# Hybrid decoder block with 32 experts: eight weight buffers over the merged activations, expert outputs as 128 rows of 1024

## The chip, the cores and the metric
The kernel runs on one core of a Trainium2 chip. Its time is the device time of one execution in microseconds, median of several runs. The core has five engines with queues of their own: TensorE (PE, with its weight loads as PEld), VectorE (DVE), ScalarE (ACT), GpSimd (POOL) and SyncE (SP), which here only issues DMA transfers. Sixteen DMA engines move data between HBM and SBUF.

## The reference
Input x has 512 tokens of width 2048, in float32. The block computes, in this order:

```
xn = rmsnorm(x);  proj = xn @ w_in
fox = forgetting attention (8 heads of 128);  ret = retention (8 heads of 128), group norm, gated
merged = sum over the two branches of sigmoid(gates) * (branch @ w_branch)
h = x + merged @ w_out
hn = rmsnorm(h)
group = argmax of 4 group logits; in it, the top 2 of 8 experts; weights = p_group * normalised top 2
moe[token] = sum over its 2 experts of weight * ((silu(hn @ w1[e]) * (hn @ w3[e])) @ w2[e])
out = rmsnorm(h + moe)
```

There are 32 experts. w1[e] and w3[e] are 2048 x 512, w2[e] is 512 x 2048, all float32: 12.58 MB for one expert, 402.7 MB for all.

## The kernel before, in words
The first part works through 60 pieces of 2 MB of dense weights, two "units" of 128 x 2048 at a time: a load of 2 MB into one of two `raw` buffers, a split of each unit by ACT and DVE into a rounded high part and the rest (`split`, two buffers named `whl`), three matmuls for each pair of tiles. The last dense product is `merged @ w_out` (L594 to L596). It goes over four column groups c of 512; in each over four quarters g of the inner dimension, then over the four token tiles. Its other operand are the merged activations `mh[k]` and `ml[k]`, k = 0 to 15, 32 tiles of 2 KB per partition at the right end of SBUF. Quarter g uses k = 4g to 4g + 3; the last column group is c = 3. Beside it and behind it run the residual, the transposes and the router's logits (tiles `hc`, `hh`, `hl`, `wrs`, `lg`), and then a chain of small DVE operations that gives each token its experts and its place (`rank1`).

The experts follow (loop from L882), each with 64 slots for tokens. `prep(e)` gathers an expert's tokens with matmuls by a 0/1 matrix S (L714 `ax`, L724 `gp`) and writes `xs`. `gemm1(e)` multiplies them by w1 (rows 0 to 63 of `ab`) and w3 (rows 64 to 127) in two halves g; each half needs two pieces of 2 MB. It then scales, transposes (`tr`) and gates to `gs`. `gemm2(e)` takes two pieces of w2: for each it runs 32 / 2 = 16 recorded matmuls into a PSUM tile `y`, and copies its two halves of 64 rows by ACT (L800) and DVE (L798) into `ysb`, 64 rows of 2048, of which there is one. GpSimd then scatters the rows by an indirect DMA to `ybuf` in DRAM (L803). The program's order is gemm1(0), prep(1), gemm1(1), prep(2), gemm2(0), gemm1(2), and so on; the last expert's gemm2 is not scattered but weighted and kept as `ys`, rounded part and rest.

A planner orders the instructions of PE, DVE, ACT and POOL by modelled times, so that work whose operands it expects early is drawn ahead; SP alone keeps the order of the program. All expert pieces are loaded from SP at L811, each into the next of seven buffers in a fixed cycle: two `raw`, three `r0` to `r2` (pool `raw2`), two `whl`. A load waits until the last reader of what its buffer overlays is done, and all that is behind it on SP waits too. `raw2` lies in space that the router's tiles used before.

At the end `combine` loads `ybuf` in four pieces of 2 MB (L918), for which the last scatter must have landed, adds the residual, the weighted rows and the last expert by matmuls (L930 to L933) and DVE (L934, L937), normalises and stores (L954). `fw` is the final norm's weight, spread over the partitions; `dgs` (L904) holds diagonal matrices of weights and shares a tile with `ab`. A loop for experts with more than 64 tokens stands behind it.

Of the kernel before, what the change touches and what calls it, by code (L numbers as in the profile page):

```python
# [30 lines left out]
DE = 512  # L31
SLOTS = 64
MAXBLK = 15
NR2 = 3
EPS = 1e-6
NEG = -1e30
ROPE_BASE = 10000.0
# [90 lines left out]
def hybrid_block(ctx, tc, a, out):  # L128
# [330 lines left out]
    scA.close()  # L459
    scM = ExitStack()  # L460
    mp = scM.enter_context(pool("mT", 1, side="right", reuse_waits="tile"))
    mh = [mp.tile([P, T], F32R, name=f"mh{j}") for j in range(KT)]
    ml = [mp.tile([P, T], F32R, name=f"ml{j}") for j in range(KT)]
    with pool("mtmp", 2, reuse_waits="tile") as mt:
        for j in range(KT):
            hi, lo = unit("br", j, after=done[3] if j == 1 else None)
            gs, bs = [], []
            for n in range(2):
# [4 lines left out]
                for k in range(H):  # L473
# [28 lines left out]
    br = rp[0].tile([P, NR], F32, name="br")  # L502
    nc.gpsimd.dma_start(br, bcast_rows(a["b_router"], 0, NR))
    tok2 = rp[0].tile([P, NT], F32, name="tok2")
    nc.gpsimd.iota(tok2, pattern=[[2 * P, NT]], base=0, channel_multiplier=0,
                   allow_small_or_imprecise_dtypes=True)
    par2 = rp[0].tile([P, NT], F32, name="par2")
    nc.gpsimd.iota(par2, pattern=[[0, NT]], base=0, channel_multiplier=2,
                   allow_small_or_imprecise_dtypes=True)
    aux = rp[0].tile([P, NT, 40], BF, name="aux")  # L510
    nc.gpsimd.memset(aux[:, :, 5:8], -4096.0)
    nc.gpsimd.tensor_copy(aux[:, :, 3], tok2)
    nc.gpsimd.tensor_copy(aux[:, :, 4], par2)

# [176 lines left out]


    cp = scC.enter_context(pool("cx", 2, reuse_waits="tile"))
    raw2 = scC.enter_context(pool("raw2", 1, reuse_waits="tile"))
    slots = [(raw, "wraw")] * 2 + [(raw2, f"r{i}") for i in range(NR2)] + [(split, "whl")] * 2
    loads = itertools.cycle(slots)

    def buffer(shape=(P, 4096)):

        pl, tag = next(loads)  # L700
        return pl.tile(list(shape), F32, name="wraw", tag=tag)

    gathering = []

    def prep(rsel, is2, eng, late=False):

        S = cp.tile([P, NT, P], BF, name="S")
        for t in range(NT):
            i = eng.tensor_scalar(S[:, t], slot1.rearrange("p a b -> p (a b)"), rsel[:, t:t + 1], None,  # L709
                                  op0=OP.is_equal)  # L710
        gathering.append(i.ins)
        ax = psY.tile([P, 40], F32, name="ax", tag="y")
        for t in range(NT):
            nc.tensor.matmul(ax, S[:, t], aux[:, t], start=(t == 0), stop=(t == NT - 1))  # L714
        rs = cp.tile([P, 1], F32, name="rs", bufs=3)
        nc.vector.reduce_sum(rs, ax[:, 0:3], axis=AX.X)
        xs = cp.tile([P, KT, SLOTS], F32, name="xs")
        for g in range(2):
            ks = slice(8 * g, 8 * g + 8)
            gp = psG.tile([P, 8, SLOTS], F32, name="gp")  # L720
            for d in range(8):
                for t in range(NT):
                    for i in range(3):
                        nc.tensor.matmul(gp[:, d], h3[i][:, t, (8 * g + d) * P:(8 * g + d + 1) * P],  # L724
                                         S[:, t, :SLOTS], start=(t == 0 and i == 0),
                                         stop=(t == NT - 1 and i == 2))
            nc.vector.tensor_mul(xs[:, ks], gp, b3(nfw[:, ks, None], 8, SLOTS))  # L727
        if late:
            ws = psY.tile([P, 3], F32, name="ws", tag="y")
# [12 lines left out]
        nc.vector.reduce_sum(ix, ax[:, 3:6], axis=AX.X)  # L742
        nc.vector.scalar_tensor_tensor(idx, ix, 4096.0, is2(ax[:, 8:40]), op0=OP.add, op1=OP.add)
        return xs, rs, idx

    def halves_mm(acc, st, w, first, last):
# [25 lines left out]
    last_ins = []  # L772
    yp = []

    def gemm2(blk, pieces, late=False, ysb=None):

        gs, idx = blk
        if late:
            wsl, sT = idx
            ys = yp[0].tile([P, D], F32R, name="ys", tag="ysb")  # L780
        elif ysb is None:
            ysb = yp[0].tile([SLOTS, D], F32, name="ysb")
        for q in range(2):
            w = next(pieces)
            y = psY.tile([P, DE], F32, name="y")
            for k in range(4):
                halves_mm(y, gs[:, k], [w[:, (4 * m + k) * DE:(4 * m + k + 1) * DE] for m in range(2)],
                          k == 0, k == 3)
            for m in range(2):
                ym = y[m * SLOTS:(m + 1) * SLOTS]  # L790
                cs = slice((2 * q + m) * DE, (2 * q + m + 1) * DE)
                if late:
                    yt = cp.tile([SLOTS, DE], F32, name="yt", tag="xs")
                    nc.scalar.activation(yt, ym, AF.Copy, scale=wsl[m * SLOTS:(m + 1) * SLOTS])
                    nc.scalar.copy(ys[:SLOTS, cs], yt)
                    nc.vector.tensor_sub(ys[SLOTS:, cs], yt, ys[:SLOTS, cs].bitcast(F32))
                elif m:
                    nc.vector.tensor_copy(ysb[:, cs], ym)  # L798
                else:
                    nc.scalar.copy(ysb[:, cs], ym)  # L800
        if late:
            return sT, ys
        nc.gpsimd.indirect_dma_start(  # L803
            out=ybuf, out_offset=IndirectOffsetOnAxis(ap=idx[:SLOTS, :1], axis=0),
            in_=ysb, in_offset=None, bounds_check=2 * T - 1, oob_is_err=False)

    def pieces_of(we, part):

# [72 lines left out]
    prev = None  # L881
    for e in range(NE):  # L882
        if e == NE - 1:
            fw = yp[0].tile([P, D], F32, name="fw")
            gemm2(prev, pieces_of(a["wM"][e - 1], 1))
            spread_fw(fw)
        cur = gemm1(x0, pieces_of(a["wM"][e], 0))
        if e == 8:
            with tc.issue_after(last_ins[-1].ins):
                nblk, eid, sta, en, it = extra_blocks()  # L890
        if e == 12:
            with tc.issue_after(last_ins[-1].ins):
# [12 lines left out]
        return dgs  # L905

    dgs = diagonals()
    sT, ys = gemm2(prev, pieces_of(a["wM"][NE - 1], 1), True)


    yv = ybuf.rearrange("(t p k) d -> t p k d", p=P, k=2)
# [48 lines left out]
    with tc.If(n_extra > 0):  # L960
        with tc.For_i(0, n_extra, 1):
            ind, tmp, e1, base = f("ind", NE), f("tmp", NE), f("e1", 1), f("base", 1)
            nc.vector.tensor_scalar(ind, sta, it, None, op0=OP.is_le)
            nc.vector.tensor_scalar(tmp, en, it, None, op0=OP.is_gt)
            nc.vector.tensor_mul(ind, ind, tmp)
            nc.vector.tensor_mul(tmp, ind, iota32)
            nc.vector.reduce_sum(e1, tmp, axis=AX.X)
            nc.vector.tensor_copy(eid, e1)
            nc.vector.tensor_mul(tmp, ind, sta)
            nc.vector.reduce_sum(base, tmp, axis=AX.X)  # L970
            nc.vector.tensor_sub(base, it, base)
            nc.vector.tensor_scalar(base, base, 1.0, float(SLOTS), op0=OP.add, op1=OP.mult)
            rsel, tmp4 = f("rsel", NT), f("tmp4", NT, NE)
            nc.vector.tensor_mul(tmp4, rank1, b3(ind[:, None, :], NT, NE))
            nc.vector.reduce_sum(rsel, tmp4, axis=AX.X)
            nc.vector.tensor_scalar(rsel, rsel, base, None, op0=OP.subtract)
            nc.vector.tensor_scalar_add(it, it, 1.0)

            def is2(c):
                nc.vector.tensor_mul(tmp, c, ind)  # L980
                r = cp.tile([P, 1], F32, name="is2")
                nc.vector.reduce_sum(r, tmp, axis=AX.X)
                return r

            ev = nc.values_load(eid[0:1, 0:1], engines=[mybir.EngineType.SP], min_val=0, max_val=NE - 1)

            we = a["wM"][ds(ev, 1)].rearrange("e q p n -> (e q) p n")
            gemm2(gemm1(prep(rsel, is2, nc.vector), pieces_of(we, 0)), pieces_of(we, 1), False, buffer((SLOTS, D)))
        combine(diagonals())
    scC.close()  # L990

# [69 lines left out]
```

## Time and profile before
| what | value |
|---|---|
| median of 3 runs | 2466.49 us (2464.05 to 2470.78) |
| profiled execution | 2463.99 us, its span 2462.3 us |
| mean granted TensorE clock | 0.989 |
| PE busy | 2374.6 us (96%) |
| DVE, ACT, POOL busy | 735.9, 484.8, 232.9 us |
| HBM read, written | 562.72 MB, 37.24 MB |
| expert loads | 192 of 2048 KB, median 22.4 us from issue to landing |

The span begins with the first instruction of the profiled execution; all times below count from there. Rows of the profile name a line (L749), an engine, an operation and `output<-input` by the program's tile names. An engine's idle time is put down to what ended it, after `<-`. In the strips of 40 slices each digit is a share in tenths; a slice is 61.6 us.

### The profile page before, as it was taken

The numbers are of one execution on the slowest core, as the hardware profiler recorded it, in microseconds if no ns is written. First come the engines' busy times: TensorE is split into PE (matmuls) and PEld (weight loads), VectorE is DVE, ScalarE is ACT, GpSimd is POOL, SyncE is SP. The second block draws the span as 40 slices with busy tenths as digits, with TensorE's granted clock in tenths as the row PEclk, the third lists the DMA queues.
The fourth block names the chain that finished last, engine by engine and source line by source line (L and its number), as shares of the span: only waits on it lengthen the run. The fifth ranks groups of instructions, "written<-read, shape, count | busy, mean of one in ns | idle before, by whom it ended". The sixth has DMA issues, their size and how long they took to land. (4 is left out here: it accounts for less than half of the span.)

```text
span 2462.3 us, 36017 instructions
## 1 busy us (share of the span) xinstructions
PE 2374.6 (96%) x16110; PEld 1618.9 (66%) x16114; DVE 735.9 (30%) x1269; ACT 484.8 (20%) x617; POOL 232.9 (9%) x328
## 2 busy tenths in 40 slices
PE   8999999999999999999999979999999999999896
PEld 6888888888888888888888855544444444444332
DVE  4444445544452222244433231111111111111105
ACT  5222222222222222232223210000001000000003
POOL 0000000100000000000003121111111111111002
PEclk9999999999999999999999989999999999999998
DMA  7233333222223333244432369999999999999995
GB/s 291 96 107 129 107 104 136 82 107 73 107 80 126 128 124 127 102 147 154 146 125 94 128 286 425 382 424 426 427 425 426 426 427 426 426 425 426 426 410 219
DMA packets 69455, 594.22 MB, mean 241 GB/s; under 512 B 7800, under 2 KB 24248, under 8 KB 34640
## 3 DMA queue, kind: packets, MB, share of 16 engines
q1 hardware_dynamic: 40320, 549.48, 54.6%
q0 software_dynamic: 7856, 25.61, 3.1%
q10 hardware_dynamic: 21120, 16.78, 2.1%
q8 instruction: 128, 2.10, 0.3%
q14 instruction: 31, 0.25, 0.0%
HBM read 562.72 MB, written 37.24 MB: 244 GB/s over the span
## 5 line engine op out<-in xcount | busy, mean ns | idle before, releaser
L749 PE MATMUL ab<-wraw,xs 128*64 128x512 f32 x2048 | 490.7, 602 | 26.8 <-DMA wraw<-in_wM_dram 26.8
L226 PE MATMUL acc<-xh,whl 128*128 128x512 f32 x1152 | 453.8, 394 | 0.0
L228 PE MATMUL acc<-xh,whl 128*128 128x512 f32 x1152 | 453.7, 394 | 0.0
L227 PE MATMUL acc<-xl,whl 128*128 128x512 f32 x1152 | 453.3, 393 | 0.0
L97 ACT CAST whl<-wraw 128x2048 fp32r<-128x2048 f32 (+1 forms) x122 | 228.1, 1869 | 780.4 <-PE acc L228 412.4
L749 PEld LDWEIGHTS ab<-wraw,xs 128*64 128x64 f32 x2048 | 150.3, 138 | 312.6 <-issue 272.9
L98 DVE TENSOR_TENSOR whl<-wraw,whl 128x2048 fp32r<-128x2048 f32 (+1 forms) x122 | 275.3, 2257 | 202.0 <-ACT whl L97 201.7
L749 PE MATMUL y<-wraw,gs 128*64 128x512 f32 x1024 | 270.1, 599 | 1.7 <-DVE gs L769 0.9
L227 PEld LDWEIGHTS acc<-xl,whl 128*128 128x128 f32 x1152 | 216.5, 188 | 46.4 <-issue 1.4
L228 PEld LDWEIGHTS acc<-xh,whl 128*128 128x128 f32 x1152 | 216.5, 188 | 46.0 <-issue 1.4
L226 PEld LDWEIGHTS acc<-xh,whl 128*128 128x128 f32 x1152 | 216.6, 188 | 45.3 <-issue 0.5
L724 PEld LDWEIGHTS <-h 128*128 128x128 bf16 x6144 | 186.7, 98 | 31.3 <-issue 30.2
L724 PE MATMUL gp<-S,h 128*128 128x64 bf16 x6144 | 191.4, 194 | 12.9 <-issue 12.9
L749 PEld LDWEIGHTS y<-wraw,gs 128*64 128x64 f32 x1024 | 85.6, 137 | 137.5 <-issue 134.3
L727 DVE TENSOR_TENSOR xs<-gp,nfw 128x512 f32<-128x512 f32 x64 | 41.8, 687 | 406.5 <-PE ab L749 368.2
L709 POOL TENSOR_SCALAR S<-slot,rank 128x128 bf16<-128x128 f32 x124 | 73.1, 600 | 707.0 <-PE ax L714 632.0
L762 ACT ACTIVATE ab<-ab,rs 128x512 f32<-128x512 f32 x32 | 22.0, 687 | 503.9 <-PE ab L749 486.1
L243 PE MATMUL acc<-whl,xh 128*128 128x512 f32 x256 | 101.6, 401 | 6.1 <-ACT xh L202 6.1
L244 PE MATMUL acc<-whl,xh 128*128 128x512 f32 x256 | 102.4, 400 | 1.0 <-DVE whl L98 1.0
L594 PE MATMUL acc<-whl,mh 128*128 128x512 f32 x256 | 100.6, 393 | 0.0
L595 PE MATMUL acc<-whl,mh 128*128 128x512 f32 x256 | 100.3, 392 | 0.0
L478 PE MATMUL acc<-oh,whl 128*128 128x512 f32 x256 | 99.5, 390 | 0.6 <-DVE whl L86 0.6
(300 smaller groups left out, 2057.3 us busy)
## 6 DMA issues: line engine op xcount, KB each, us to landing
wraw<-in_wM_dram SPq DMA_DIRECT2D x192, 2048.0 KB, 22.4
wraw<-in_wA_dram SPq DMA_DIRECT2D x59, 2048.0 KB, 7.9
ybuf<-zero ACTq DMA_DIRECT2D x8, 1024.0 KB, 5.9
gate<-gs ACTq DMA_DIRECT2D x32, 256.0 KB, 2.0
g<-gate POOLq DMA_DIRECT2D x32, 256.0 KB, 3.0
wraw<-ybuf SPq DMA_DIRECT2D x4, 2048.0 KB, 14.4
xt<-in_x_dram SPq DMA_DIRECT2D x4, 1024.0 KB, 6.7
hc<-in_x_dram POOLq DMA_DIRECT2D x4, 1024.0 KB, 5.5
```

Of the source, the lines that this page charges most:

```text
L97: nc.scalar.copy(hi[:, c], w[:, c])
L98: nc.vector.tensor_sub(lo[:, c], w[:, c], hi[:, c].bitcast(F32))
L226: nc.tensor.matmul(acc, wh, xh[:, k], start=(k == 0), stop=False)
L227: nc.tensor.matmul(acc, wh, xl[:, k], start=False, stop=False)
L228: nc.tensor.matmul(acc, wl, xh[:, k], start=False, stop=(k == KT - 1))
L243: nc.tensor.matmul(accs[t], xh[:, k, s], wh, start=(k == 0), stop=False)
L244: nc.tensor.matmul(accs[t], xh[:, k, s], wl, start=False, stop=False)
L478: nc.tensor.matmul(b, wl, oh[i], start=False, stop=(k == H - 1))
L594: nc.tensor.matmul(accs[t], mh[k][:, s], wh, start=(k == 0), stop=False)
L595: nc.tensor.matmul(accs[t], mh[k][:, s], wl, start=False, stop=False)
L724: nc.tensor.matmul(gp[:, d], h3[i][:, t, (8 * g + d) * P:(8 * g + d + 1) * P], S[:, t, :SLOTS], start=(t == 0 and i == 0), stop=(t == NT - ...
L749: nc.tensor.matmul(acc[m * SLOTS:(m + 1) * SLOTS], st, w[m], start=first, stop=last)
```

## The change
The seven buffers become eight: `raw2` gets four buffers, placed at the right end over `mh` and `ml`, and the cycle is r3, r2, r1, raw, raw, r0, whl, whl. The merged activations are allocated from the last to the first, so that r3 lies over k = 0 to 3, r2 over 4 to 7, r1 over 8 to 11 and r0 over 12 to 15. `fw` and `ys` are each taken from this cycle for good before the last two experts, and six buffers are left for the loads behind.

`gemm2` takes both of its pieces first. Piece m holds the columns from 1024 m on, and `y` number q now has in its rows 0 to 63 columns of piece 0 and in rows 64 to 127 columns of piece 1. One copy of 128 x 512 each (ACT for q = 0, DVE for q = 1) fills `ysb`, 128 rows of 1024, and the scatter writes 128 rows of 4 KB where it wrote 64 of 8 KB; its row numbers are made for both halves. `is2`, `tok2` and `par2` are scaled for that, and `rowbase` adds the half's number.

```diff
-    mh = [mp.tile([P, T], F32R, name=f"mh{j}") for j in range(KT)]
-    ml = [mp.tile([P, T], F32R, name=f"ml{j}") for j in range(KT)]
+    mh, ml = ([None] * KT for _ in range(2))
+    for j in reversed(range(KT)):
+        mh[j] = mp.tile([P, T], F32R, name=f"mh{j}")
+        ml[j] = mp.tile([P, T], F32R, name=f"ml{j}")
...
-    raw2 = scC.enter_context(pool("raw2", 1, reuse_waits="tile"))
-    slots = [(raw, "wraw")] * 2 + [(raw2, f"r{i}") for i in range(NR2)] + [(split, "whl")] * 2
-    loads = itertools.cycle(slots)
-
-    def buffer(shape=(P, 4096)):
-
-        pl, tag = next(loads)
-        return pl.tile(list(shape), F32, name="wraw", tag=tag)
+    raw2 = scC.enter_context(pool("raw2", 1, side="right", reuse_waits="tile"))
+    loads = itertools.cycle([(raw2, "r3"), (raw2, "r2"), (raw2, "r1"), (raw, "wraw"), (raw, "wraw"), (raw2, "r0"),
+                             (split, "whl"), (split, "whl")])
+    kept = set()
+    for i in range(4):
+        raw2.tile([P, 4096], F32, name="wraw", tag=f"r{i}")
+
+    def buffer(shape=(P, 4096), dtype=F32, keep=False):
+
+        pl, tag = next(x for x in loads if x[1] not in kept)
+        if keep:
+            kept.add(tag)
+        return pl.tile(list(shape), dtype, name="wraw", tag=tag)
...
-        nc.vector.scalar_tensor_tensor(idx, ix, 4096.0, is2(ax[:, 8:40]), op0=OP.add, op1=OP.add)
+        nc.vector.tensor_add(ix, ix, rowbase)
+        nc.vector.scalar_tensor_tensor(idx, is2(ax[:, 8:40]), 2.0, ix, op0=OP.mult, op1=OP.add)
...
-    def gemm2(blk, pieces, late=False, ysb=None):
+    def gemm2(blk, pieces, ys=None):
...
-            ys = yp[0].tile([P, D], F32R, name="ys", tag="ysb")
-        elif ysb is None:
-            ysb = yp[0].tile([SLOTS, D], F32, name="ysb")
+        else:
+            ysb = yp[0].tile([P, 2, DE], F32, name="ysb")
+        w = [next(pieces), next(pieces)]
         for q in range(2):
-            w = next(pieces)
             y = psY.tile([P, DE], F32, name="y")
             for k in range(4):
-                halves_mm(y, gs[:, k], [w[:, (4 * m + k) * DE:(4 * m + k + 1) * DE] for m in range(2)],
-                          k == 0, k == 3)
+                ws = slice((4 * q + k) * DE, (4 * q + k + 1) * DE)
+                halves_mm(y, gs[:, k], [w[m][:, ws] for m in range(2)], k == 0, k == 3)
+            if ys is None:
+                if q:
+                    nc.vector.tensor_copy(ysb[:, q], y)
+                else:
+                    nc.scalar.copy(ysb[:, q], y)
+                continue
...
         nc.gpsimd.indirect_dma_start(
-            out=ybuf, out_offset=IndirectOffsetOnAxis(ap=idx[:SLOTS, :1], axis=0),
-            in_=ysb, in_offset=None, bounds_check=2 * T - 1, oob_is_err=False)
+            out=ybuf.rearrange("r (m n) -> (r m) n", m=2),
+            out_offset=IndirectOffsetOnAxis(ap=idx[:, :1], axis=0),
+            in_=ysb.rearrange("p q n -> p (q n)"), in_offset=None, bounds_check=4 * T - 1, oob_is_err=False)
...
         if e == NE - 1:
-            fw = yp[0].tile([P, D], F32, name="fw")
+            fw = buffer((P, D), F32, True)
+            ys = buffer((P, D), F32R, True)
             gemm2(prev, pieces_of(a["wM"][e - 1], 1))
```

## Rows read from the trace of the kernel before
**Rows 1.** The page: TensorE's busy time; DMA engines' share and rate in 40 slices

```profile
PE 2374.6 (96%) x16110; PEld 1618.9 (66%) x16114; DVE 735.9 (30%) x1269; ACT 484.8 (20%) x617; POOL 232.9 (9%) x328
...
DMA  7233333222223333244432369999999999999995
GB/s 291 96 107 129 107 104 136 82 107 73 107 80 126 128 124 127 102 147 154 146 125 94 128 286 425 382 424 426 427 425 426 426 427 426 426 425 426 426 410 219
```

**Rows 2.** Stretches: each engine's busy us, then granted clock, DMA share, GB/s

```profile
1437.00:1457.00 20.00, 14.79 (x241) 10.10 (x243) 6.78 (x28) 0.00 (x0) 4.87 (x8) 0.77 1.00 425
1540.00:1580.00 40.00, 40.00 (x522) 20.66 (x520) 4.18 (x9) 2.11 (x4) 5.63 (x9) 1.00 0.90 358
1700.00:2000.00 300.00, 288.90 (x2979) 135.00 (x2977) 42.58 (x126) 24.94 (x45) 32.93 (x50) 1.00 1.01 426
...
2390.00:2405.00 15.00, 13.95 (x61) 4.53 (x58) 0.23 (x1) 1.41 (x3) 0.00 (x0) 0.94 0.63 267
```

**Rows 3.** Waits of SP's queue, 1370 to 1500: total us, times, longest

```profile
SPq L811 <- DVE hl L554: 27.6, 1, 27.6
```

**Rows 4.** Expert loads (L811) in 1378:1434, 1434:1450, 1450:1470; landing in 1370:1500

```profile
L811 SPq DMA_DIRECT2D wraw<-in_wM_dram x2: 327/328/328, 1378.8 to 1404.3; - x2
...
L811 SPq DMA_DIRECT2D wraw<-in_wM_dram x5: 327/383/644, 1434.5 to 1436.6; - x5
...
L811 SPq DMA_DIRECT2D wraw<-in_wM_dram x4: 328/353/384, 1457.1 to 1464.4; - x4
...
DMA to landing us min/median/max: 7.6/13.6/26.3
```

**Rows 5.** L596, last column group, quarters 1, 2 and 4: first and last start

```profile
L596 PE MATMUL acc<-whl,ml x16: 388/390/396, 1387.8 to 1398.9; 128*128 128x512 f32 x16
L596 PE MATMUL acc<-whl,ml x16: 388/390/390, 1399.6 to 1409.8; 128*128 128x512 f32 x16
L596 PE MATMUL acc<-whl,ml x17: 388/390/401, 1410.5 to 1422.3; 128*128 128x512 f32 x17
```

**Rows 6.** Timeline of PE, first experts: start us, us, what, count

```profile
1450.03 13.95 PE L749 MATMUL ab<-wraw,xs 128*64 128x512 f32 x64
...
1470.17 13.96 PE L749 MATMUL ab<-wraw,xs 128*64 128x512 f32 x64
...
1491.71 6.23 PE L749 MATMUL y<-wraw,gs 128*64 128x512 f32 x28 [0.30 <-issue]
```

**Rows 7.** The gather's matmuls (L724) alone in two stretches of 30 us

```profile
1540.00:1570.00 30.00, 12.58 (x396) 11.96 (x396) 1.00 0.90 366
1600.00:1630.00 30.00, 5.76 (x192) 5.74 (x192) 1.00 1.00 422
```

**Rows 8.** PE's groups, 1600 to 2300: busy, mean ns, idle before

```profile
L749 PE MATMUL y<-wraw,gs 128*64 128x512 f32 x736 | 197.3, 596 | 0.4 <-issue 0.4
```

**Rows 9.** DMA queues in 1600:2300, 2437:2462, 1000:1300: packets, MB, share

```profile
q0 software_dynamic: 1920, 6.05, 2.1%
...
q1 hardware_dynamic: 1152, 4.19, 42.4%
...
q0 software_dynamic: 2944, 9.75, 10.5%
```

**Rows 10.** Timelines of POOL, ACT, DVE and PE near the end

```profile
2405.16 2.35 POOL L904 TENSOR_SCALAR dgs<-ident,wt 128x128 f32<-128x128 f32 x4 [30.53 <-PE tr L765]
2407.68 0.93 POOL L803 DMA_INDIRECT ybuf<-ysb,idx  x1 [0.17 <-issue]
...
2404.18 1.04 ACT L800 COPY ysb<-y 64x512 f32<-64x512 f32 x2
...
2404.77 1.30 DVE L798 COPY ysb<-y 64x512 f32<-64x512 f32 x2 [31.32 <-ACT ysb L800]
...
2420.77 0.75 DVE L934 SCALAR_TENSOR_TENSOR wraw<-wraw,wt,ab 128x512 f32<-128x512 f32 x1 [3.34 <-DMA wraw<-ybuf]
...
2406.58 7.09 PE L749 MATMUL y<-wraw,gs 128*64 128x512 f32 x32 [0.95 <-DVE gs L769]
```

More of the change, by code (lines that the diff above doesn't have):

```diff
@@ L33 @@
 MAXBLK = 15
-NR2 = 3
 EPS = 1e-6
@@ L504, in hybrid_block @@
     tok2 = rp[0].tile([P, NT], F32, name="tok2")
-    nc.gpsimd.iota(tok2, pattern=[[2 * P, NT]], base=0, channel_multiplier=0,
+    nc.gpsimd.iota(tok2, pattern=[[4 * P, NT]], base=0, channel_multiplier=0,
                    allow_small_or_imprecise_dtypes=True)
     par2 = rp[0].tile([P, NT], F32, name="par2")
-    nc.gpsimd.iota(par2, pattern=[[0, NT]], base=0, channel_multiplier=2,
+    nc.gpsimd.iota(par2, pattern=[[0, NT]], base=0, channel_multiplier=4,
                    allow_small_or_imprecise_dtypes=True)
     aux = rp[0].tile([P, NT, 40], BF, name="aux")
-    nc.gpsimd.memset(aux[:, :, 5:8], -4096.0)
+    nc.gpsimd.memset(aux[:, :, 5:8], -8192.0)
     nc.gpsimd.tensor_copy(aux[:, :, 3], tok2)
@@ L693, in hybrid_block @@
     cp = scC.enter_context(pool("cx", 2, reuse_waits="tile"))
-    raw2 = scC.enter_context(pool("raw2", 1, reuse_waits="tile"))
-    slots = [(raw, "wraw")] * 2 + [(raw2, f"r{i}") for i in range(NR2)] + [(split, "whl")] * 2
-    loads = itertools.cycle(slots)
-    def buffer(shape=(P, 4096)):
-        pl, tag = next(loads)
-        return pl.tile(list(shape), F32, name="wraw", tag=tag)
+    raw2 = scC.enter_context(pool("raw2", 1, side="right", reuse_waits="tile"))
[9 more added lines that the diff above has]
+        return pl.tile(list(shape), dtype, name="wraw", tag=tag)
     gathering = []
+    rowbase = rp[0].tile([P, 1], F32, name="rowbase")
+    nc.gpsimd.memset(rowbase[:SLOTS], 8192.0)
+    nc.gpsimd.memset(rowbase[SLOTS:], 8193.0)
     def prep(rsel, is2, eng, late=False):
@@ L773, in hybrid_block @@
     yp = []
-    def gemm2(blk, pieces, late=False, ysb=None):
+    def gemm2(blk, pieces, ys=None):
         gs, idx = blk
-        if late:
+        if ys is not None:
             wsl, sT = idx
-            ys = yp[0].tile([P, D], F32R, name="ys", tag="ysb")
-        elif ysb is None:
-            ysb = yp[0].tile([SLOTS, D], F32, name="ysb")
+        else:
+            ysb = yp[0].tile([P, 2, DE], F32, name="ysb")
+        w = [next(pieces), next(pieces)]
         for q in range(2):
-            w = next(pieces)
@@ L789, in gemm2 @@
             for m in range(2):
                 ym = y[m * SLOTS:(m + 1) * SLOTS]
[L791 to L800, printed above, removed]
@@ L801, in gemm2 @@
-        if late:
-            return sT, ys
+                cs = slice((2 * m + q) * DE, (2 * m + q + 1) * DE)
+                yt = cp.tile([SLOTS, DE], F32, name="yt", tag="xs")
+                nc.scalar.activation(yt, ym, AF.Copy, scale=wsl[m * SLOTS:(m + 1) * SLOTS])
+                nc.scalar.copy(ys[:SLOTS, cs], yt)
+                nc.vector.tensor_sub(ys[SLOTS:, cs], yt, ys[:SLOTS, cs].bitcast(F32))
+        if ys is not None:
+            return sT
         nc.gpsimd.indirect_dma_start(
-            out=ybuf, out_offset=IndirectOffsetOnAxis(ap=idx[:SLOTS, :1], axis=0),
-            in_=ysb, in_offset=None, bounds_check=2 * T - 1, oob_is_err=False)
+            out=ybuf.rearrange("r (m n) -> (r m) n", m=2),
+            out_offset=IndirectOffsetOnAxis(ap=idx[:, :1], axis=0),
+            in_=ysb.rearrange("p q n -> p (q n)"), in_offset=None, bounds_check=4 * T - 1, oob_is_err=False)
@@ L907, in hybrid_block @@
     dgs = diagonals()
-    sT, ys = gemm2(prev, pieces_of(a["wM"][NE - 1], 1), True)
+    sT = gemm2(prev, pieces_of(a["wM"][NE - 1], 1), ys)
     yv = ybuf.rearrange("(t p k) d -> t p k d", p=P, k=2)
@@ L972, in hybrid_block @@
             nc.vector.tensor_scalar(base, base, 1.0, float(SLOTS), op0=OP.add, op1=OP.mult)
-            rsel, tmp4 = f("rsel", NT), f("tmp4", NT, NE)
+            rsel, tmp4 = f("rsel", NT), oh1.rearrange("p t g j -> p t (g j)")
             nc.vector.tensor_mul(tmp4, rank1, b3(ind[:, None, :], NT, NE))
@@ L987, in hybrid_block @@
             we = a["wM"][ds(ev, 1)].rearrange("e q p n -> (e q) p n")
-            gemm2(gemm1(prep(rsel, is2, nc.vector), pieces_of(we, 0)), pieces_of(we, 1), False, buffer((SLOTS, D)))
+            gemm2(gemm1(prep(rsel, is2, nc.vector), pieces_of(we, 0)), pieces_of(we, 1))
         combine(diagonals())
```

## The prediction
> **What bounds the kernel now.** I read the page's first two parts first. TensorE is busy for 96% of the span, but the DMA strip says more: about 1420 of the 2462 us have the DMA engines at two to four tenths, and from slice 24 on (each is 61.6 us) they stand at 9 and move 425 GB/s [rows 1]. So there are two kernels in one: dense projections bound by TensorE, then the experts, bound by the load of their weights. An expert's six loads are 12.58 MB and its rows written to ybuf about 0.26 MB (1024 rows of 8 KB over 32 experts); at 426 GB/s that is 30.2 us, of which TensorE is idle for 1.1 us (288.9 of 300 us busy, over 300 / 30.2 = 9.9 experts) [rows 2]. All that the change can win lies at the start of this stream, in a hole of it, or behind it.
>
> The start: two expert loads leave early (1378.8 and 1404.3 us, into `raw`), then the in-order SP queue stands behind `r0`, which overlays a tile of the router (27.6 us on `hl` L554), and five loads leave together at 1434.5 to 1436.6 [rows 3, 4]. The first experts' matmuls begin at 1450.0, set by the router's chain and by the gather, not by weights: 64 `ab` matmuls run without a gap [rows 6]. The hole: from 1540 to 1580 the rate is 358 GB/s, while TensorE is 100% busy, so there the loads wait for buffers that TensorE is late to free [rows 2]. TensorE is late because two gathers are drawn ahead: 396 `gp` matmuls in 30 us there, 192 in a usual stretch [rows 7].
>
> **The change part by part.** *The first eight loads.* `r3`, `r2`, `r1`, `r0` now lie over the merged activations. These are used up by quarters of the last output column group; the last matmul of each quarter starts at 1387.8, 1399.6, 1410.5 and 1422.3 us [rows 5]. SP issues in order, so loads 0 and 1 leave at about 1388 and 1400, loads 2 to 4 at 1410.5 (`raw` is free by 1404.3), loads 5 to 7 at 1422.5. A first load takes 7.6 us [rows 4], each behind it 2.097 MB / 426 GB/s = 4.92 us. The last six have landed at 1410.5 + 7.6 + 5 x 4.92 = 1442.7 us, before the first use at 1450.0. TensorE starts no earlier for it. What is won is that load 8 is next when the first buffers come free, at 1457.1 us, halfway through expert 0 [rows 4]. It lands at 1457.1 + 7.6 = 1464.7. Today load 8 is the seventh of the stream that begins at 1434.5: 1434.5 + 7.6 + 6 x 4.92 = 1471.6. **Gain 6.9 us**, not the 50 us by which the first load moves. Of it some is lost again, since a dry queue follows: load 12 needs a buffer of the first half of expert 1, free at 1470.2 + 14.0 / 2 = 1477.2, and lands at 1484.8 where an unbroken stream had it at 1464.7 + 4 x 4.92 = 1484.4; load 16 needs one of `y` of expert 0, free at 1497.9 [rows 6], and lands at 1505.5 where the stream has it at 1484.8 + 4 x 4.92 = 1504.5. **Lost 0.4 + 1.0 = 1.4 us.**
>
> *Eight buffers for seven.* In the hole 40 us x (426 - 358) / 426 = 6.4 us of transfer are missing. One buffer more lets DMA run 4.92 us further ahead of TensorE, but `gemm2` now takes both of its pieces before its first matmul and holds both until its last, some 4 us longer for the first one. Bounds: nothing kept, all 6.4 us. I take **3.5 us**, a little over half, because the order in which gathers are drawn ahead should come later, when TensorE has caught up.
>
> *Both pieces ahead of `y`.* In 700 us of the steady stretch the 736 `y` matmuls waited 0.4 us in all, and for no DMA [rows 8]: both pieces lie there when `y` begins. Cost nothing; cover gone if `y` moves up against its landing.
>
> *Outputs as 128 rows of 1024.* Four copies of 64x512 become two of 128x512. ACT and DVE are idle for most of this stage (in 300 us 24.9 and 42.6 busy [rows 2]), so nothing is won on the path; the same holds for the added `tensor_add` on `ix`, one small DVE operation per expert. The scatter moves the same bytes in 4 KB rows. In the stream today's 8 KB rows go at 6.05 MB / (2.1% of 16 x 700 us) = 25.7 GB/s per engine; the 4 KB rows of the output store at 4.19 MB / (42.4% of 16 x 25 us) = 24.7, and 4 KB rows of the GpSimd queue amid other loads at 9.75 MB / (10.5% of 16 x 300 us) = 19.3 [rows 9]. A scatter's 0.61 us of all engines thus becomes 0.64 to 0.81; times 31 that is 0.8 to 6.3 us. A gain is excluded, as the bytes are the same and the mixed stream already moves them at its full rate [rows 2]. Nearest is the store, also out of SBUF: **cost 1.1 us**.
>
> *`fw` and `ys` in kept buffers.* For the last two experts six buffers are left. Each load there waits for a buffer used by the piece six before it; about three loads are then still in flight, so DMA does not run dry; 0 to 4.9 us, I take 0.
>
> *The end.* Today the scatter of expert 30 leaves only at 2407.7, since on GpSimd it stands behind `dgs`, which waits for expert 31's transposes, and its last copies on ACT come at 2404.2, behind expert 31's `ab`; DVE's copies had waited 31.3 us for ACT's. The loads of ybuf wait for that scatter, and the first final DVE operation starts at 2420.8 [rows 10]. If this order stays, the end keeps its length but for one copy fewer (1.04 us for two): **gain 0.5 us**. The other order is a rival.
>
> Sum: 6.9 - 1.4 + 3.5 - 1.1 + 0.5 = 8.4 us. The profiled execution took 2463.99 us, 1.7 us of it outside the span, so it would be 2455.6; it lies 2.5 us under the median of the runs shown, 2466.49. Against the median: **2458 us**.
>
> **The rivals.**
> *(a) The end is reordered.* `ys` no longer shares the tile of `ysb`, and one ACT copy goes. If expert 30's copies and scatter run when its `y` is there, up to 31 us sooner, the ybuf loads queue right behind the weights and fill DMA, which falls to 267 GB/s from 2390 to 2405 [rows 2]. Then the last stage waits for `ys`: `y` starts at 2406.6 [rows 10], its first half takes 3.6, scaling, rounding and subtraction 3.9, so DVE starts at about 2415 in place of 2420.8, 5.8 us: 2452. For it: nothing but order holds the scatter. Against: the scatter still waits for both copies, the copies for the one `ysb` tile that the scatter before reads, and `dgs` for what it waits for now.
> *(b) The gain is not made.* Either SP waits for the whole of the merged activations, so that all eight loads leave at 1422.5: load 8 lands eighth behind, 1422.5 + 7.6 + 8 x 4.92 = 1469.5, 4.8 us worse than forecast; or the hole stays as it is and the scatter costs its upper bound (3.5 + 5.2 us). 2463 to 2467. For it: the pairs held longer. Against: rows 5, where quarters are used up one after another.
> *(c) Slower: `y` as one unit makes TensorE the bound.* This is the case on the other side. If TensorE is made to wait for the second piece ahead of `y`, it has nothing to put in its place where the order is fixed. It decides from 1.1 us per expert, TensorE's idle time [rows 2]; each us beyond is 31 us. At 2 us: 0.9 x 31 = 28 us, 2486. For it: TensorE is the second bound by a hair. Against: `y` never waits for DMA now [rows 8].
> [...]
>
> **How the numbers follow.** Forecast 0.52 (own range 2453 to 2463), (a) 0.20, (b) 0.15, (c) 0.09, (d) 0.04. A change under 0.3% (7.4 us) can't be told from none in this kernel, so faster means under 2459.1: six tenths of the forecast's chance, nearly all of (a), and (d): 0.54. Slower means over 2473.9: (c) alone, and a tail of (b): 0.10. The rest, 0.36, is within. The range takes in (a) below with some room, and (b) above with the scatter's and the last buffers' upper bounds: 2447 to 2471.
>
> **What would show it.** Eight expert loads issued by about 1423; none between then and about 1457; then 426 GB/s; the stretch 1540 to 1580 above 358; the first `ab` matmul still at about 1450; the first final DVE operation 8 to 9 us sooner than at 2420.8, with the scatter of expert 30 behind `dgs` as now, or 14 us sooner with the scatter ahead of it. I am wrong if the first loads stay together at 1422 or later, if DMA falls below 426 in the steady stretch, if `y` waits for a DMA, or if TensorE's first expert moves.

## The result

The changed kernel takes 2638.32 us (median; 2632.9 to 2641.0) against 2466.9 us of the kernel before on the same chip: ratio 1.0691, 95% interval 1.0668 to 1.0714, or 171 us slower. The prediction, 2458 us in a range of 2447 to 2471, was wrong.

The page of the changed kernel: TensorE's busy time, then the DMA engines' share and rate in 40 slices.

```profile
PE 2433.3 (92%) x16114; PEld 1625.7 (62%) x16114; DVE 716.1 (27%) x1269; ACT 468.4 (18%) x586; POOL 235.3 (9%) x330
...
DMA  7233333222233333444326868898888789788896
GB/s 288 72 133 103 122 113 109 108 73 96 100 120 120 120 121 122 152 144 145 112 80 271 362 284 336 336 388 351 349 348 344 323 350 374 324 333 343 374 383 284
```

The row of nines of [rows 1] is gone: from slice 24 to the last but one (65.9 us each here) DMA moves 323 to 388 GB/s. The stretches of [rows 2] (columns as there) say the same, and that TensorE lost with it:

```profile
1437.00:1457.00 20.00, 14.72 (x241) 9.80 (x243) 7.35 (x31) 0.00 (x0) 4.79 (x8) 0.79 0.29 121
1540.00:1580.00 40.00, 39.18 (x351) 16.74 (x349) 2.90 (x8) 1.66 (x3) 3.39 (x5) 1.00 0.75 310
1700.00:2000.00 300.00, 256.64 (x2506) 114.40 (x2507) 31.22 (x113) 15.61 (x28) 30.42 (x45) 0.95 0.86 356
2000.00:2300.00 300.00, 245.43 (x2431) 109.86 (x2428) 21.37 (x64) 12.38 (x24) 27.12 (x40) 0.97 0.83 344
```

Neither resource is full: 256.64 of 300 us on TensorE (288.90 before) and 356 GB/s (426). Two things that take turns wait for each other. The loads show how. Expert loads (L822, issue of the first and last, and count) in 1380 to 1440, 1450 to 1460, 1950 to 1985 and 1985 to 2020:

```profile
L822 SPq DMA_DIRECT2D wraw<-in_wM_dram x8: 327/352/561, 1388.6 to 1424.1; - x8
...
L822 SPq DMA_DIRECT2D wraw<-in_wM_dram x2: 328/352/377, 1456.8 to 1457.2; - x2
DMA to landing us min/median/max: 7.9/10.1/12.3
...
L822 SPq DMA_DIRECT2D wraw<-in_wM_dram x6: 328/430/639, 1953.1 to 1955.7; - x6
...
L822 SPq DMA_DIRECT2D wraw<-in_wM_dram x6: 328/446/548, 1989.6 to 1992.1; - x6
```

The start is as forecast: eight loads by 1424.1, the next at 1456.8, landing 7.9 us later at 1464.7. In the stream, six loads leave within 2.6 us and then none for 34; one expert takes 36.5 us in place of 30.2. The timeline of PE across one such period (start us, us, what, count):

```profile
1952.47 0.63 PE L759 MATMUL y<-wraw,gs 128*64 128x512 f32 x2
1953.03 0.27 PE L723 MATMUL ax<-aux,S 128*128 128x40 bf16 x4
...
1967.43 8.78 PE L759 MATMUL ab<-wraw,xs 128*64 128x512 f32 x32 [1.70 <-DMA wraw<-in_wM_dram]
1977.38 7.08 PE L759 MATMUL ab<-wraw,xs 128*64 128x512 f32 x30 [1.16 <-DMA wraw<-in_wM_dram]
1985.29 0.66 PE L775 MATMUL tr<-ident,ab 128*128 128x128 f32 x4 [0.83 <-ACT ab L772]
1986.00 3.65 PE L759 MATMUL y<-wraw,gs 128*64 128x512 f32 x16
1989.59 0.27 PE L723 MATMUL ax<-aux,S 128*128 128x40 bf16 x4
1990.70 0.19 PE L733 MATMUL gp<-S,h 128*128 128x64 bf16 x1 [0.84 <-POOL S L718]
1990.82 1.51 PE L759 MATMUL y<-wraw,gs 128*64 128x512 f32 x6
```

The 16 `y` matmuls at 1986.0 and those from 1990.8 on are not the two halves of one expert. The first are the second column group (q = 1) of one expert, the others the first group (q = 0) of the next. In the planned order q = 1 stands behind the whole of the next expert's `gemm1`. Both pieces of w2 serve both groups, so both buffers stay held until then, and eight loads later one of them is wanted again: the load at 1989.6 leaves as the `y` at 1986.0 ends. What fills the period is a chain: burst at 1953.1; the fourth piece lands 24.2 us later, at 1977.3; half of `gemm1` 7.1; transposes and gate 1.6; half of `y` 3.6; next burst at 1989.6. The first half of `gemm1`, at 1967.43, takes 8.78 us for 32 records where 7.1 is usual: behind 1.70 us in which TensorE stood idle, the granted clock was 0.51 from 1967.7 to 1971.1. That half ends 1.16 us before the fourth piece lands, so in this period it does not set the time. The waits (us in total, times, longest):

```profile
SPq L822 <- PE ax L723: 852.0, 27, 36.9
...
PE ab L759 <- DMA wraw<-in_wM_dram: 113.8, 57, 3.6
...
DVE idx L753 <- DMA ybuf<-ysb,idx: 25.6, 4, 10.9
```

SP is held 27 times, up to 36.9 us; the release is put down to `ax`, the instruction just behind q = 1. The last line is the first trace of why: `idx` has waited for a scatter to be done.

### The profile page after: what moved, and what is told of

It reads as the page before. It is cut to its first block, busy times and chain, and to the rows that moved or that the text cites. A ratio compares the mean times of both kernels' runs of the same rounds, so it can differ in the third digit from the quotient of the medians.

```text
span 2637.9 us, 35885 instructions
## 1 busy us (share of the span) xinstructions
PE 2433.3 (92%) x16114; PEld 1625.7 (62%) x16114; DVE 716.1 (27%) x1269; ACT 468.4 (18%) x586; POOL 235.3 (9%) x330
## 5 line engine op out<-in xcount | busy, mean ns | idle before, releaser
L759 PE MATMUL ab<-wraw,xs 128*64 128x512 f32 x2048 | 524.7, 636 | 113.8 <-DMA wraw<-in_wM_dram 113.8
L759 PEld LDWEIGHTS ab<-wraw,xs 128*64 128x64 f32 x2048 | 156.6, 146 | 430.5 <-issue 287.6
L759 PE MATMUL y<-wraw,gs 128*64 128x512 f32 x1024 | 244.7, 606 | 3.8 <-ACT ysb L802 1.2
L733 PE MATMUL gp<-S,h 128*128 128x64 bf16 x6144 | 199.3, 194 | 25.2 <-POOL S L718 20.9
L759 PEld LDWEIGHTS y<-wraw,gs 128*64 128x64 f32 x1024 | 77.0, 139 | 145.7 <-issue 112.6
L596 PE MATMUL acc<-whl,mh 128*128 128x512 f32 x256 | 100.4, 392 | 0.0
## 6 DMA issues: line engine op xcount, KB each, us to landing
wraw<-in_wM_dram SPq DMA_DIRECT2D x192, 2048.0 KB, 18.5
wraw<-ybuf SPq DMA_DIRECT2D x4, 2048.0 KB, 15.1
```

The costliest lines, as they stand in the source:

```text
L596: nc.tensor.matmul(accs[t], mh[k][:, s], wl, start=False, stop=False)
L759: nc.tensor.matmul(acc[m * SLOTS:(m + 1) * SLOTS], st, w[m], start=first, stop=last)
```

## The experiments

Where the time goes is read below from four points: the landing of load 29 (the last of the first 30), of load 173 and of load 191 (the last), counted from 0 as in the prediction, and the end of the span. Each row is one profiled execution, and executions of the kernel before alone lie between 2463.0 and 2470.8 us; one or two us in a single cell are not clear of that. The table gives each stretch against the kernel before, whose points are 1585.0, 2314.6, 2406.1 and 2462.3.

| kernel | time us | to load 29 | 29 to 173 | 173 to 191 | 191 to end | sum |
|---|---|---|---|---|---|---|
| changed | 2638.3 | +15.1 | +160.4 | +6.3 | -6.2 | +175.6 |
| four index tiles | 2463.2 | +0.1 | +2.7 | +2.5 | -5.0 | +0.3 |
| the same, q = 1 behind q = 0 | 2457.9 | -1.1 | +2.5 | +0.4 | -9.6 | -7.8 |
| the same, one piece per group | 2456.8 | -4.5 | +3.1 | +0.1 | -6.3 | -7.6 |
| four index tiles, late loads | 2462.9 | -0.5 | +2.7 | +2.7 | -4.9 | 0.0 |
| one piece per group, late loads | 2457.5 | -4.7 | +2.9 | +0.1 | -6.3 | -8.0 |
| one piece per group, seven buffers | 2464.5 | +3.9 | +0.9 | +1.3 | -5.6 | +0.5 |
| one piece per group, three index tiles, `ax` elsewhere | 2457.5 | -2.7 | +3.9 | 0.0 | -5.0 | -3.8 |
| seven buffers | 2470.7 | +6.5 | +3.6 | +2.7 | -7.0 | +5.8 |
| rows and pair on the kernel before | 2470.0 | +7.1 | +2.2 | -0.6 | -2.8 | +5.9 |
| `ys` alone on the kernel before | 2457.8 | -0.1 | +0.7 | +0.6 | -8.0 | -6.8 |

**Why `y` is late: four index tiles.** `ax` and the two `y` groups take turns in two PSUM buffers. The buffer that q = 1 gets was last `ax`'s, and its last reader is `idx`, which needs one of three index tiles, that is an older scatter out of the way.

```
-        ix = cp.tile([P, 1], F32, name="ix", bufs=3)
-        idx = cp.tile([P, 1], I32, name="idx", bufs=3)
+        ix = cp.tile([P, 1], F32, name="ix", bufs=4)
+        idx = cp.tile([P, 1], I32, name="idx", bufs=4)
```

> The changed kernel with four index tiles (ix, idx) in place of three; the planned order of TensorE then has both halves of an expert's y ahead of the next expert's matmuls. Theory (order): the loss of 171 us comes from the second half of y, which the planner put behind the next expert's gemm1, so that both w2 buffers stay taken one expert longer; here 2450 to 2462 us, DMA near 426 GB/s in the steady stretch. Rival 1 (pair): holding two pieces in gemm2 costs it by itself; about 2630. Rival 2 (rows): the scatter of 128 rows of 4 KB slows the transfers; about 2630.

Measured: 2463.24 us, ratio 0.9990 (0.9980 to 0.9999). The 171 us are gone with one more tile of 128 x 1 each for `ix` and `idx`, which puts `y` back into one turn, so the order was the cause; but the time is 1 us above the range expected. TensorE, 1700 to 2000, and its timeline over one period:

```profile
1700.00:2000.00 300.00, 299.99 (x2952) 137.23 (x2950) 37.98 (x124) 19.58 (x34) 33.95 (x50) 1.00 1.01 424
```

```profile
1922.37 1.88 PE L759 MATMUL y<-wraw,gs 128*64 128x512 f32 x4
1924.18 0.66 PE L775 MATMUL tr<-ident,ab 128*128 128x128 f32 x4
1924.67 0.98 PE L733 MATMUL gp<-S,h 128*128 128x64 bf16 x28
1925.59 7.08 PE L759 MATMUL y<-wraw,gs 128*64 128x512 f32 x28
1932.60 0.67 PE L733 MATMUL gp<-S,h 128*128 128x64 bf16 x17
...
1952.72 1.88 PE L759 MATMUL y<-wraw,gs 128*64 128x512 f32 x4
```

TensorE is now full, and `y` is why. Its two output halves (64 rows each) can run beside each other: in the kernel before the 16 records from 1917.07 on take 3.65 us and start in twos 5 to 7 ns apart, from the second two on every 0.43 us. Here two matmuls of the first half (`x4`) are drawn ahead by themselves: four records take 1.81 us, 1922.37 to 1924.18, one every 0.43. The halves left over at the end of the 28 run alone too. An expert's `y` takes 20 steps of 0.43 us where 16 would do. In the kernel before, `y` is split as well, but about half of its split records start beside one of `ab`: counted over 1700 to 2000, `ab` and `y` together take 50.1 steps per expert there and 53.9 here.

**The late order alone.** Four index tiles, and q = 1 forced behind the next expert's transposes:

```
+                with tc.issue_after(turned_ins[-1]) if q else nullcontext():
+                    halves_mm(y, gs[:, k], [w[m][:, ws] for m in range(2)], k == 0, k == 3)
```

> As e1 with four index tiles, but the second half of each expert's y is put behind the next expert's transposes by an explicit order on TensorE, which is the order that the changed kernel has. Theory (order): 2620 to 2650 us, loads in bursts of six, 36 to 37 us per expert. Rival 3 (index tile on the chip): the wait of the index for an older scatter costs the time on the chip itself, not by the order; then as e1, 2450 to 2470.

Measured: 2662.43 us, ratio 1.0802 (1.0784 to 1.0820). The order by itself costs all of it: 12 us more than the range expected and 24 more than the changed kernel, so the forced order is not quite the planned one. With four index tiles its trace has no wait of `idx` for a scatter, so that wait on the chip is not what costs the time.

**Seven buffers.** The tile `r0` left out of the cycle; everything else as changed. With it the planned order keeps `y` in one turn, with three index tiles.

> The changed kernel with seven buffers (r0 left out, cycle r3 r2 r1 raw raw whl whl), three index tiles; gemm2, the pair of pieces, and the 128 rows as in the change. Its planned order has the two halves of y ahead of the next gemm1 but for its first matmuls. Theory (order): 2458 to 2472 us. Rivals 1 and 2 (pair, rows): with one buffer fewer and the same pair and rows no better than the changed kernel, 2630 or more.

Measured: 2470.65 us, ratio 1.0024 (1.0015 to 1.0034). Neither the pair of pieces nor the rows of 1024 are what costs 171 us. Nor do three index tiles and the shared PSUM buffers always put q = 1 late: both are here too.

**One piece per column group, order still late.** The layout of w2 in DRAM is changed so that group q needs one piece, as before the change:

```
-        w = [next(pieces), next(pieces)]
         for q in range(2):
+            w = next(pieces)
...
-    wm[:, 4:6] = s.transpose(0, 3, 2, 4, 1, 5).reshape(NE, 2, P, 2, 2048)
+    wm[:, 4:6] = s.transpose(0, 4, 2, 3, 1, 5).reshape(NE, 2, P, 2, 2048)
```

> The changed kernel with w2 laid out so that each half of y needs one piece alone: the pieces are taken and freed one by one, eight buffers and 128 rows as in the change. Its planned order still has the second half of y behind the next gemm1. Theory (order): the second load of the next expert still waits for it, 2580 to 2640 us. Rival 1 (pair): without the pair 2450 to 2470. Rival 2 (rows): about 2630.

Measured: 2524.01 us, ratio 1.0245 (1.0228 to 1.0262): between the two, as neither expected. Of the late order's 171 us about 59 come with one held piece per expert (DMA 393 and 399 GB/s in the two stretches from 1700 and 2000), the rest with the second: it is the pair that makes the late order dear.

**Pairing.** Four index tiles, and q = 1 issued behind q = 0, so that one `y` matmul is drawn ahead and not two:

```
-                halves_mm(y, gs[:, k], [w[m][:, ws] for m in range(2)], k == 0, k == 3)
+                with tc.issue_after(mm) if q else nullcontext():
+                    mm_ = halves_mm(y, gs[:, k], [w[m][:, ws] for m in range(2)], k == 0, k == 3)
+            mm = mm_
```

> The changed kernel with four index tiles, and the second column group of y issued behind the first: one y matmul is drawn ahead in place of two. With four index tiles alone TensorE was busy for 300.0 of 300 us, and of an expert's y matmuls the profile showed only part starting in pairs 7 ns apart (both halves of the output beside each other); a lone one takes the same 0.43 us as a pair, so y took 20 such steps per expert against 18 now. Theory (lost pairing made TensorE the bound and ate what the early loads won): 0.86 us of TensorE per expert come free, DMA is the bound again in the stretch 1700 to 2000, TensorE idle there by 0.3 to 1 us per expert, 2453 to 2460 us. Rival (the two pieces held for the whole of y limit the loads, whatever the pairing): 2462 to 2465, TensorE idle more, DMA no faster between 1540 and 1580.

Measured: 2457.88 us, ratio 0.9971 (0.9960 to 0.9981). The stretches 1700 to 2000 and 2000 to 2300:

```profile
1700.00:2000.00 300.00, 299.88 (x2981) 136.04 (x2979) 37.92 (x124) 19.56 (x34) 34.86 (x52) 1.00 1.01 426
2000.00:2300.00 300.00, 295.06 (x2956) 136.50 (x2954) 30.43 (x80) 16.55 (x30) 33.88 (x50) 1.00 1.01 426
```

The time came as the theory said, but the table says where: the stretch from load 29 to 173 is the same as without the edit (+2.5, +2.7). `ab` and `y` take 52.0 steps per expert, but TensorE was still full until 2000, idle only later than expected. What shrank is what follows load 173, by 2.1 + 4.6 us; why the last 4.6 came was not taken apart.

**One piece per group, in order.** The layout above with four index tiles.

> The changed kernel with four index tiles, and the second matrix laid out so that each column group of y needs one piece alone, as before the change. Eight buffers, early loads and rows of 1024 stay. Theory: both halves of every y matmul start together (16 steps of 0.43 us per expert in place of 20), pieces come free one at a time, TensorE has over 1 us of idle per expert, and the gain of the first loads (6.9 us) and of the eighth buffer is kept: 2449 to 2458 us. Rival (nothing but the weight stream and its start set the time, and these are the same with four index tiles alone): 2462 to 2465.

Measured: 2456.76 us, ratio 0.9967 (0.9955 to 0.9979), the lowest median of all, a third of a per cent under the kernel before. By the table 6.3 of its 7.6 us lie behind the last load.

**Late loads.** Four index tiles; `r0`, used up last, taken first, so that all eight loads leave together:

```
-    loads = itertools.cycle([(raw2, "r3"), (raw2, "r2"), (raw2, "r1"), (raw, "wraw"), (raw, "wraw"), (raw2, "r0"),
+    loads = itertools.cycle([(raw2, "r0"), (raw2, "r2"), (raw2, "r1"), (raw, "wraw"), (raw, "wraw"), (raw2, "r3"),
```

> The changed kernel with four index tiles, and the tiles over the merged activations taken in the opposite order, so that the first load waits for the quarter that is used up last and all eight leave at about 1422. Everything behind is as with four index tiles alone (2463.2). Theory (there TensorE is the bound from the second expert on, so the time at which the loads arrive counts little): 2463 to 2466. Rival (the stream of loads is the bound, so load 8 behind an unbroken stream costs the 4.8 us that the prediction gave it): 2467 to 2469.

Measured: 2462.89 us against 2463.24; the eight loads left from 1423.2 to 1426.8. Their intervals overlap (0.9977 to 0.9995, 0.9980 to 0.9999): the early loads win nothing here that can be told.

**Rows and pair on the kernel before.** Its buffers and first loads; gemm2, index arithmetic and scatter as changed. `ys` also has a tile of its own here, not that of `ysb`.

> The kernel before with its seven buffers and their order, and of the change only the 128 rows of 1024 with their index arithmetic, and both pieces taken ahead of y. Theory (the order of the changed kernel, not the rows or the pair, cost the 171 us; with seven buffers y stays in one expert's turn): 2464 to 2472, by 0 to 6 us of scatter. Rival (rows of 4 KB at half the rate of 8 KB, 0.6 us of all engines for each scatter more): 2485. Beside the run with seven buffers and the early start (2470.65) it gives what the early start is worth there: by the prediction 4 to 7 us, so this one at 2474 to 2478.

Measured: 2469.97 us, ratio 1.0019 (1.0010 to 1.0028), 4.8 us slower. Most of what it loses goes in 1460 to 1540 (first the kernel before, then this run), some in 1540 to 1580, 358 GB/s in [rows 2]:

```profile
1460.00:1540.00 80.00, 79.70 (x1025) 42.08 (x1022) 10.09 (x25) 6.81 (x11) 9.01 (x14) 1.00 1.01 425
...
1460.00:1540.00 80.00, 78.87 (x1014) 41.60 (x1012) 9.23 (x27) 5.67 (x9) 9.21 (x14) 1.00 0.95 396
1540.00:1580.00 40.00, 40.00 (x517) 20.62 (x515) 3.46 (x9) 1.66 (x3) 5.72 (x9) 1.00 0.82 334
```

That is 5.4 and 2.3 us of transfer at 426 GB/s. With seven buffers the pair and the rows together delay the stream by 7.1 us before load 29 and by 2.2 in the 24 experts after; which of the two does it, this run does not say. And the early start on top of it (2470.65) gives nothing back, where 4 to 7 us were expected.

**The end alone.** The kernel before with `ys` in a load buffer that is kept, as in the change, and nothing else:

```
-            ys = yp[0].tile([P, D], F32R, name="ys", tag="ysb")
+            ys = ysb
...
+            ys = buffer((P, D), F32R, True)
             gemm2(prev, pieces_of(a["wM"][e - 1], 1))
```

> The kernel before with one part of the change alone: ys, the scaled output of the last expert, in a load buffer of its own that is kept, in place of the tile that it shared with ysb. Seven buffers, first loads, rows of 2048 as before. Theory (with the order mended the whole gain lies at the end: the scatter of expert 30 runs before dgs, and the loads of ybuf are there when the last y is): first final DVE operation 3 to 6 us sooner than at 2420.8, and less time behind it; 2456 to 2461 us. Rival (the gain comes from the early loads and the eighth buffer): 2464 to 2468.

Measured: 2457.78 us, ratio 0.9969 (0.9957 to 0.9981). Timelines of POOL, SP and DVE at its end, to be read against [rows 10]:

```profile
2384.47 0.90 POOL L807 DMA_INDIRECT ybuf<-ysb,idx  x1 [11.45 <-DVE ysb L802]
2406.26 2.36 POOL L909 TENSOR_SCALAR dgs<-ident,wt 128x128 f32<-128x128 f32 x4 [20.89 <-PE tr L769]
...
2396.41 8.59 SPq L923 DMA_DIRECT2D wraw<-ybuf  x4
...
2417.55 0.75 DVE L939 SCALAR_TENSOR_TENSOR wraw<-wraw,wt,ab 128x512 f32<-128x512 f32 x1
```

The scatter of expert 30 leaves at 2384.5, not 2407.7, ahead of `dgs`; the loads of `ybuf` begin at 2396.4, and the first final DVE operation comes at 2417.6 in place of 2420.8. From there to the end it is 37.9 us (2417.55 to 2455.5) against 41.5 (2420.77 to 2462.3). The four loads land 7.6 to 8.2 us sooner, the first at 2412.2 in place of 2420.4, and TensorE need not wait for it (first the kernel before):

```profile
2420.48 2.05 PE L932 MATMUL ab<-wraw,dgs 128*128 128x512 f32 x2 [4.16 <-DMA wraw<-ybuf]
...
2416.24 1.02 PE L937 MATMUL ab<-wraw,dgs 128*128 128x512 f32 x2
```

Behind that wait of 4.16 us the granted clock was 0.50 from 2420 to 2425; the two records take 2.05 us there and 1.02 in this run. The four L934 operations of the first token tile end 6.6 us after the first of them begins; here (L939) it is 3.5 us, which is 3.1 of the 3.6. This one part of the change is worth as much as the whole change in its best form (2457.8 and 2456.8).

**Late loads where TensorE has room.** The fastest kernel with the late cycle.

> The kernel with four index tiles and one piece for each column group of y (2456.8), its first loads made late: the tiles over the merged activations in the opposite order, so that all eight leave at about 1422. Theory (from the second expert to about 1700 us TensorE is 100% busy, loads wait for the buffers that it frees, so what the first loads win is gone by the fourth expert): 2455 to 2459. Rival (the prediction's 4.8 us between this and the early order): 2460 to 2463.

Measured: 2457.53 us, ratio 0.9969 (0.9958 to 0.9980), like the 0.9967 of the early order. Loads in 1450 to 1470 (landing) and 1536 to 1600, then SP's waits in 1460 to 1600; first the early order:

```profile
DMA to landing us min/median/max: 7.8/12.0/16.3
...
L822 SPq DMA_DIRECT2D wraw<-in_wM_dram x12: 327/328/367, 1543.9 to 1593.6; - x12
...
SPq L822 <- PE ab L759: 82.1, 12, 14.3
```

then the late order:

```profile
DMA to landing us min/median/max: 14.3/18.0/21.7
...
L822 SPq DMA_DIRECT2D wraw<-in_wM_dram x12: 327/328/372, 1543.7 to 1593.4; - x12
...
SPq L822 <- PE ab L759: 82.1, 12, 14.6
```

The early order has load 8 on the chip 5.8 us sooner (1464.9, 1470.7). But the loads from 1543 on leave at the same time in both, because they wait for buffers that TensorE frees, and TensorE works from 1450 on without a pause to speak of (79.68 of 80 us in 1460 to 1540 in the early order, 79.17 in the late). Load 24 lands at 1552.4 and 1552.3.

**Seven buffers, one piece per group.**

> The kernel with four index tiles and one piece for each column group of y (2456.8), with seven load buffers in place of eight (the tile r0 left out). Theory (an eighth buffer buys nothing, since the hole between 1540 and 1580 is as deep with it as without): 2455 to 2460. Rival (the prediction's 3.5 us for the hole): 2459 to 2463.

Measured: 2464.45 us, ratio 0.9996 (0.9987 to 1.0005): 7.7 us slower than with eight, more than the rival had. In this kernel the eighth buffer counts: load 29 lands at 1588.9, with eight at 1580.5. The theory that it buys nothing was wrong.

**`ax` out of the buffers of `y`.** One piece per group, three index tiles:

```
-        ax = psY.tile([P, 40], F32, name="ax", tag="y")
+        ax = psR.tile([P, 40], F32, name="ax", tag="tr")
```

> The changed kernel with one piece for each column group of y, three index tiles as in the change, and ax taken out of the two PSUM buffers of y. Theory (y was held back because its second column group took the PSUM buffer whose last reader waits for an index tile): the column groups stand in one expert's turn again though the index tiles are three, and the time is that with four index tiles: 2454 to 2460. Rival (three index tiles hold the stream by themselves, through the scatter they wait for): 2500 or more, like 2524 with ax among the buffers of y.

Measured: 2457.53 us, ratio 0.9965 (0.9952 to 0.9979), against 2524.01 with `ax` among the buffers of `y`. So with eight buffers it is the shared PSUM buffer together with the three index tiles that puts q = 1 late; either edit mends it. Which modelled times made the planner choose so was not read.

## Why the prediction was wrong

**Both pieces ahead of `y`: the step that failed.** "In 700 us of the steady stretch the 736 `y` matmuls waited 0.4 us in all, and for no DMA [rows 8]: both pieces lie there when `y` begins. Cost nothing; cover gone if `y` moves up against its landing." It asked only what `y` waits for, not who waits for `y`. Both column groups now read both pieces, so the pieces come free only when the last matmul of q = 1 is done, and nothing bound q = 1 to q = 0. It moved back by a whole `gemm1`, and the loads waited for it: 36.5 us per expert in place of 30.2. One of its signs of being wrong came: DMA below 426 GB/s in the steady stretch (356). The forecast had the hold as "some 4 us longer"; the trace has 32 (the first piece would have come free with q = 0, 1957.9, and does with q = 1, 1989.6). Rival (c) had the right part of the change, `y` as one unit, at a chance of 0.09; its mechanism, TensorE waiting for the second piece, was not it: `y` still waits for no DMA. With the order mended TensorE did become full, by lone halves, at some 6 us (2463.2 for 2456.8).

**The first eight loads.** The issue times (1388.6 to 1424.1 for 1388 to 1422.5), load 8 (1464.7 for 1464.7) and the first `ab` (1449.7 for 1450) were right. That this gain reaches the end was not: early or late first loads made no difference in two pairs of kernels (2463.2 and 2462.9; 2456.8 and 2457.5). The sum treated load 8 as the head of a stream with nothing but DMA in its way, though the same text said that in the hole TensorE is the bound. The lead of the loads over a busy TensorE was spent once loads waited for buffers: 5.8 us at load 8, none by load 24 (1552.4 and 1552.3).

**Eight buffers.** 3.5 us were put on the hole, and the term was mis-sized. In the fastest kernel the hole is as deep as before (346 GB/s for 358), yet load 29 lands 4.5 us sooner. The same kernel with seven buffers has load 29 8.4 us later and takes 7.7 us more: there the eighth buffer is worth twice the forecast. But that kernel is also 3.9 us behind the kernel before at load 29; which part of the change costs these 3.9 us no run shows.

**Outputs as 128 rows.** 1.1 us was the forecast (the rate of the store, which it names as the nearest, gives 0.8 by its own sum). The scatter's queue in 1600 to 2300, in the fastest kernel and in the kernel before with rows and pair, against the first line of [rows 9]:

```profile
q0 software_dynamic: 3442, 6.00, 2.3%
...
q0 software_dynamic: 3312, 5.83, 2.2%
```

That is 23.3 and 23.7 GB/s per engine in place of 25.7, or 0.05 to 0.06 us of all engines more per scatter: an estimate of 1.6 to 2 us for 31, near the forecast and inside its bounds. In the kernels with these rows and `y` in one turn the 24 experts from load 29 to 173 take 0.9 to 3.9 us longer, in the one without them 0.7; how much of the difference is the rows' is not shown. No run shows the cheaper scatter that (d) has in the chances, at 0.04: with these rows the scatter's rate was lower, the 23.3 and 23.7 GB/s above.

**The end.** 0.5 us was forecast on the ground that the order stays; rival (a) happened. POOL and DVE at the end of the changed kernel, against [rows 10]:

```profile
2576.59 0.96 POOL L813 DMA_INDIRECT ybuf<-ysb,idx  x1 [11.88 <-DVE ysb L800]
2587.70 2.35 POOL L916 TENSOR_SCALAR dgs<-ident,wt 128x128 f32<-128x128 f32 x4 [10.16 <-PE tr L775]
...
2599.25 0.75 DVE L946 SCALAR_TENSOR_TENSOR wraw<-wraw,wt,ab 128x512 f32<-128x512 f32 x1
```

The scatter of expert 30 stands 11 us ahead of `dgs`. That gave 6.2 us even here, and 4.9 to 9.6 with the order mended, against the 5.8 that rival (a) had (its own terms, 2406.6 + 3.6 + 3.9, give 2414.1 and not 2415, so 6.7). The argument against it, that `dgs` and the scatter wait for what they wait for now, did not decide: as rival (a) said, nothing but order held the scatter, and with `ys` in a kept buffer the planner puts the scatter ahead of `dgs`, by 22 us in the kernel with that alone. That `ys` no longer shares the tile of `ysb` is not enough by itself: in the kernel before with rows and pair it has a tile of its own too, and the scatter stays behind `dgs`:

```profile
2413.80 1.78 POOL L910 TENSOR_SCALAR dgs<-ident,wt 128x128 f32<-128x128 f32 x3 [28.20 <-PE tr L769]
2415.74 1.03 POOL L807 DMA_INDIRECT ybuf<-ysb,idx  x1 [0.17 <-issue]
```

What makes the planner choose one or the other was not read.

With eight buffers, `y` in order and its halves kept together, the kernel takes 2457 to 2458 us, the very number forecast. That is luck: the forecast had 8 us from the stream and 0.5 from the end; in these kernels the stream changes by 1.8 us at most either way, and 5 to 10 us come from the end.

## What to carry to other kernels

Where a change makes two pieces of work share a buffer's lifetime, follow the buffer to its last reader in the order that the new kernel will really have, not the one of before: a planner may put the second reader anywhere that nothing forbids. A load that arrives sooner is worth something only up to the next point where loads wait for the engine that uses them (here a lead of 5.8 us at load 8 was gone by load 24); ask which of the two is full in the stretch right behind. And test the small edits by themselves: here a kept buffer for `ys`, alone, was worth the whole of a large change.

## What the runs showed of the hardware

Two matmuls into the two 64-row halves of a PSUM tile took one step of 0.43 us together where they stand next to each other, with starts 5 to 7 ns apart for the 16 `y` records from 1917.07 on in the kernel before. A lone one took the same step: with four index tiles, four of them 1.81 us. The neighbour can belong to another tile: in the kernel before, `y` and `ab` records pair in the same way (1935.821 and 1935.827 us). The 3.8 steps per expert that four index tiles add are 1.6 us; [rows 2] had left TensorE 1.1 us per expert.

In a burst of six loads the pieces land about 4.9 us apart from the fourth on (1972.4, 1977.3, 1982.2, 1987.1), and from 1957 to 1985 DMA moves 425 GB/s, the rate of the steady stream: what was lost is the time between bursts. The median from issue to landing is lower in the slow kernel (18.5 us, 22.4 before), so a short wait of a load is no sign of a fast stream.

During or behind some waits of TensorE the granted clock was half: in the changed kernel 0.51 from 1967.7 to 1971.1, behind 1.70 us of idle time from 1965.7 on, and in the kernel before 0.50 from 2419.0 to 2425.8, where TensorE waited 4.16 us from 2416.3. Behind 2.76 us of idle time that ended at 1927.68, again in the changed kernel, it was 1.00 and 32 records took 7.09 us. That the idle time brings the lower clock is not shown.
